# A two-layer backbone on one core: two PSUM banks for the by-token products, products with the gate made ahead, and longer planned steps

## The chip, the cores and the metric

One core of one Trainium2 chip runs the whole forward pass in one launch. The metric is the device time of that core in microseconds (us), lower is better. TensorE (PE) does the matrix products, VectorE (DVE) and GpSimd (POOL) the elementwise work, ScalarE (ACT) activations and copies; SyncE (SP) and ACT issue the DMAs.

## The reference, cut to what matters

The model has one even and one odd layer over 256 latent and 256 context tokens of width 2048. Everything is float32. The even layer, in which the whole change lies, is

```
p = h @ w_in                                  # 50 column blocks of 128
a, r, k, v, wd, ad, gate = split(p)
mixed = [pool_mixer(a) | rwkv7(r, k, v, wd, ad), both directions]
y = (mixed * silu(gate)) @ w_out
x = layer_norm(alpha * x + gate_l * y)
```

`rwkv7` is a recurrence over the tokens for 16 heads of 64, in both directions: S becomes S*w + (S a) b + v k, and the output is S r. The odd layer is attention with the same frame. Products of activations and weights run as three float32r matmuls (high*high, high*low, low*high) on operands that were split into a high and a low part.

## The kernel before, in words

**Matrix order.** The order of TensorE's instructions is written by a planner at build time (`merge`, line 121). Work is a set of generators with priorities. A generator that yields a number asks to go on that many planned microseconds later; one that yields another generator waits for its end. The planner keeps a planned clock `self.t`, which `mm` and `tp` move on, and always takes the first ready generator in the order of priority. The last in priority, the fill (`fill0`, line 1303), is the projection with weights that has no dependence: it runs in every planned wait of the others. The order of the other engines and of the DMA queues is chosen by the framework from its own simulated timeline.

**The fill.** `inproj` (line 321) makes one block of 128 columns of p: four units of 12 matmuls of 128x512. `run_fill` (line 183) loads the weights of a unit on SP (`load`, line 198), up to `rawbufs` - 1 units ahead, and splits them one unit ahead (`split`, line 203: ACT makes whi, POOL makes wlo). A block that is done goes to DRAM (`spill`, line 299); the 16 gate blocks pass SiLU first. The order of the blocks is r, k, v by pairs of heads, then the 8 pool blocks, then the 16 gate blocks 0 to 15.

**The recurrence** (`rwkv`, line 1272) goes through 8 passes of two heads each. `lora` (line 358) makes the decay rates once, `prep` (411) the operands of a pass, `gram` (484) the products within a chunk of 64 tokens, `inverse` (542, on DVE) and `join` (577) the inverse of a triangular block, `by_token` (504) the transposed operands and NV, and `chain` (628) the recurrence itself in 8 chunks. While `chain` of pass p runs, `prep` and `inverse` of pass p + 1 run beside it; `join` and `by_token` of p + 1 follow when the chain has ended. `readout` (675) ends a pass and writes `mixd` to DRAM; the last pass runs beside `pools` (696), the pooling mixer.

**PSUM.** There are eight banks: two each under the names acc, tr and prep, one each under cx and cz. `chain` uses cx and cz; `join`, `gram` and `by_token` share the two tr banks. A bank is given out again when all that it held has been read.

**Out-projection of the even layer** (`out0`, line 893). When the fill's blocks are done, `gate_acts` (880) makes for each of 16 blocks k, in the order `korder` (8 to 14, 0 to 7, 15), the product of `mixd` and the gate: two loads on SP, a multiplication on DVE (line 743) and a split, hh on ACT and hl on POOL (`split_act`, 76; `gated_act`, 734), in turn in the two ev tiles and in two raw tiles. `outproj` (860) runs passes of 16 units of 12 matmuls; pass 0 uses the acc and tr banks and takes block k when it is there. When pass 0 has ended, `done` (916) waits for the recurrence and calls `pools()` (897), which closes the memory pools of the recurrence and of ev, opens the larger set of weight buffers (`rawbufs` from 4 to 6) in their place and calls `loads(0)`: six DMAs of 256 KB on ACT for the layer norm. `done` then uses them and calls `loads(1)`, six more.

Of the kernel before, what the change touches and what calls it, by code (L numbers as in the profile page):

```python
# [7 lines left out]
F32 = mybir.dt.float32  # L8
F32R = mybir.dt.float32r
AF = mybir.ActivationFunctionType  # L10
ALU = mybir.AluOpType
# [3 lines left out]
KT = D // 128  # L15
# [13 lines left out]
M_A, M_R, M_K, M_V, M_WD, M_AD, M_G = 0, 8, 16, 24, 32, 33, 34  # L29
# [7 lines left out]
class Kern:  # L37
# [320 lines left out]
    def lora(self):  # L358


        nc, io = self.nc, self.io
        rows = (slice(0, 64), slice(64, 128))
        W, xh = [], [self.rt([128, 2, 512], f"AR{j}", F32R, bufs=2) for j in range(2)]
        xl = [self.rt([128, 2, 512], "BKT0", F32R), self.rt([128, 2, 512], "BK", F32R, bufs=2)]
        for j in range(2):
            nc.gpsimd.memset(xl[j][rows[1 - j]].bitcast(F32), 0.0)
        stage = [("GN0", None), ("BKT1", None), ("GR0", 2), ("GR1", 2)]
        raws = []
        for j, m in enumerate((M_WD, M_AD)):
            for d in range(2):  # L370
                t = self.rt([128, 2, 512], "M")[:, :, 0:258] if j + d == 0 else self.rt([128, 2, 512], "GN1")[:, :, 0:258] if j + d == 2 else self.rt([128, 8, 65], "P").rearrange("p a b -> p (a b)")[:, 0:516].rearrange("p (s t) -> p s t", s=2) if j else self.rt([128, 2, 258], "rsh")
                nc.gpsimd.memset(t[:, :, 0:258:257], 0.0)
                for r in rows:
                    nc.sync.dma_start(t[r, :, 1:257], self.pd[m][rows[d], :].rearrange("p (s t) -> p s t", s=2))
                raws.append(t)
        t1 = self.rt([128, 2, 512], "D")
        for j, n in enumerate(("w2", "a2")):
            hi, lo = rows[j], rows[1 - j]
            for d in range(2):
                w = self.rt([128, 1024], stage[2 * j + d][0], bufs=stage[2 * j + d][1])  # L380
                nc.scalar.dma_start(w, io[n][d])
                Wt = self.rt([128, 1024], ("X", "U0", "U1", "NV")[2 * j + d], F32R)
                W.append(Wt)
                x = self.rt([128, 512], "acc", bufs=2)
                self.shifted(raws[2 * j + d], d, self.c("mul", 2 * j + d), self.muc[:, 48 + 2 * j + d:49 + 2 * j + d], x.rearrange("p (s t) -> p s t", s=2), t1[:, d, :])
                if j == 0:
                    nc.scalar.activation(x, x, AF.Tanh)
                nc.scalar.copy(xh[j][:, d, :], x)
                nc.vector.tensor_tensor(out=xl[j][hi, d, :], in0=x[hi], in1=xh[j][hi, d, :].bitcast(F32), op=ALU.subtract)
                nc.scalar.copy(Wt, w)  # L390
                (nc.vector if d else nc.gpsimd).tensor_tensor(out=Wt[lo], in0=w[lo], in1=Wt[lo].bitcast(F32), op=ALU.subtract)
        outs = [self.rt([128, 2, 512], n, bufs=b) for n, b in (("GN0", None), ("BKT1", None), ("GN1", None), ("GR0", 2), ("GR1", 2))]
        yield 12.0
        for p in range(8):
            ps = slice(p * 128, p * 128 + 128)
            for d in range(2):
                o = outs[(2 * p + d) % 5]
                for j, b in enumerate(("w0", "a0")):
                    pw = self.pt(("prep", "tr")[j])
                    self.mm(pw, W[2 * j + d][:, ps], xh[j][:, d, :], stop=False)  # L400
                    self.mm(pw, W[2 * j + d][:, ps], xl[j][:, d, :], start=False)
                    last = nc.scalar.activation(o[:, j, :], pw, AF.Sigmoid, bias=self.c(b, d * 8 + p))
                    yield 0.2
                nc.sync.dma_start(self.sgd[p, d], o)
                self.rates += 1
        self.preload(last)
# [97 lines left out]
    def by_token(self, st):  # L504

        nc, cst = self.nc, self.cst
        st["U"] = U = [self.rt([128, 2, 8, 64], f"U{h}") for h in range(2)]
        st["BKT"] = BKT = [self.rt([128, 16, 64], f"BKT{h}") for h in range(2)]
        st["NV"] = NV = self.rt([128, 2, 8, 64], "NV")
        for d in range(2):  # L510
            pv = self.pt("tr", (128, 8, 64))
            for c in range(8):
                for h in range(2):
                    hs = slice(64 * h, 64 * h + 64)
                    os = slice(64 - 64 * h, 128 - 64 * h)
                    self.mm(pv[os, c, :], st["v"][d][hs, c * 64:c * 64 + 64], cst["cen"][hs, :], share=0.5)
            with self.tc.high_priority():
                nc.scalar.copy(U[0][64:128, d], pv[64:128])
                nc.vector.tensor_copy(U[1][0:64, d], pv[0:64])
            yield 0.5  # L520
        for d in range(2):
            pq = [self.pt("tr", (128, 8, 64)) for _ in range(2)]
            for c in range(8):
                for h in range(2):
                    hs = slice(64 * h, 64 * h + 64)
                    self.tp(pq[h][:, c, :], st["BK"][d][hs, c, :, :], cst["ident"][hs, hs], share=0.5)
            with self.tc.high_priority():
                for h in range(2):
                    (nc.scalar.copy if h else nc.vector.tensor_copy)(BKT[h][:, d * 8:d * 8 + 8, :], pq[h])
            yield 1.8  # L530
        for d in range(2):
            pn = self.pt("tr", (128, 8, 64))
            for c in range(8):
                for h in range(2):
                    ks = slice(64 - 64 * h, 128 - 64 * h)
                    os = slice(64 * h, 64 * h + 64)
                    self.mm(pn[os, c, :], st["GN"][h][ks, d * 8 + c, :], U[h][ks, d, c, :], share=0.5)
            with self.tc.high_priority():
                nc.scalar.copy(NV[:, d], pn)
            yield 1.2  # L540
# [82 lines left out]
                lo = slice(64 * h, 64 * h + 32)  # L623
                (nc.scalar.copy if h else nc.vector.tensor_copy)(X[lo, :, 1, :], px[lo])

    LAG = 1.7, 2.4, 2.2

    def chain(self, st):

# [100 lines left out]
                nc.scalar.activation(ev, ps, AF.Identity, scale=self.c("pscale", 2 * g + m))  # L730
                nc.sync.dma_start(self.mixd[2 * g + m], ev)


    def gated_act(self, k):

        nc = self.nc
        if self.korder.index(k) % 2:
            g, x = (self.ep.tile([128, 512], F32, tag="ev", name="ev") for _ in range(2))
        else:
            g, x = (self.rt([128, 2, 258], f"raw{j}").rearrange("p a b -> p (a b)")[:, 0:512] for j in range(2))  # L740
        nc.sync.dma_start(g, self.pd[M_G + k])
        nc.sync.dma_start(x, self.mixd[k])
        nc.vector.tensor_tensor(out=x, in0=x, in1=g, op=ALU.mult)
        return self.split_act(x, 512)

    def rsqrt(self, pool, out, v):

# [129 lines left out]

        return self.run_fill([unit(j, i, k) for j in range(len(passes)) for i, k in enumerate(ks)])

    def gate_acts(self):  # L880
        last = None
        for k in self.korder:
            yield self.mixed[k]
            yield from self.spilled(M_G + k)
            y = self.gated_act(k)
            yield 2.6
            if last is not None:
                self.y[last[0]] = last[1]
            last = k, y
        yield 2.0  # L890
        self.y[last[0]] = last[1]

    def out0(self, main):
        nc, io = self.nc, self.io
# [13 lines left out]
        def loads(n):  # L908
# [4 lines left out]
            for t in range(4):  # L913
                self.behind(nc.scalar.dma_start(z[t][:, w], io["xtok"][t * 128:(t + 1) * 128, w]), after)

        def done(n, toks, acc):
            if n == 0:
                yield main
                yield self.gemv_p
                pools()  # L920
            for t, a in zip(toks, acc):
                w = slice(n * 512, n * 512 + 512)
                tmp = self.ln.tile([128, 512], F32, tag="tmp", name="tmp", bufs=2)
# [23 lines left out]
        a, b = ("acc", "acc", "tr", "tr"), ("prep", "prep", "cx", "cz")  # L947
# [355 lines left out]
    def fill0(self, main):  # L1303

        right = lambda name, **kw: self.tc.tile_pool(name=name, side="right", **kw)
        rkv = [m + p for p in range(1, 8) for m in (M_R, M_K, M_V) if m + p != M_R + 1]
        yield from self.run_fill([u for m in rkv + list(range(8)) + [M_G + i for i in range(16)] for u in self.inproj(m)])
        self.act.__exit__(None, None, None)
        self.act2 = right("act2", bufs=KT)
        self.hp = self.act2.__enter__()  # L1310
        self.spawn(self.gate_acts(), 5)
        yield from self.out0(main)
        yield from self.layer1()

    def run(self, ctx):
        tc, self.ctx = self.tc, ctx
        self.joined = Proc(None, 0, 0)
        self.mixed = [Proc(None, 0, 0) for _ in range(KT)]
        self.y = [None] * KT
        self.there = set()  # L1320
        self.rates = 0
        self.bns = {}
# [2 lines left out]
        with tc.manual_schedule(engines={mybir.EngineType.PE}):  # L1325
# [5 lines left out]
            self.lo_pat = "p"  # L1331
            main = self.spawn(self.rwkv())
            self.gemv_p = self.spawn(self.gemvs(), 8)
            fill = self.spawn(self.fill0(main), 9)
            self.merge(main, fill)

# [72 lines left out]
```

## Time and profile before

| | us |
|---|---|
| median of 3 runs (lowest, highest) | 1929.61 (1924.73, 1929.91) |
| the profiled execution's own time | 1930.54 |
| its span, first to last instruction | 1928.8 |
| PE busy in it | 1734.2 (90%) |
| DVE, ACT, POOL busy | 1026.6, 730.0, 667.3 |
| mean granted clock of PE, as a share of the full one | 0.95 |

The span is what the trace shows; the profiled execution took 1.7 us more. A matmul's record lasts longer than the time after which the next one starts, so a busy PE is not yet PE at its peak; idle PE and a lower granted clock are both lost time.

### The profile page before, as it was taken

How to read it: one execution, taken by the hardware profiler on the slowest of the kernel's cores; microseconds unless marked ns; L12 is line 12 of the kernel's file. 1: busy time of each engine (PE TensorE's matmuls, PEld its weight loads, DVE VectorE, ACT ScalarE, POOL GpSimd, SP SyncE). 2: the span in 40 equal slices, each digit the busy share in tenths (PEclk: the TensorE clock that was granted, in tenths of full speed). 3: DMA queues.
4: the chain of work that ended last, by engine and by line, in shares of the span. 5: the costliest groups of instructions: out<-in, count | busy, mean ns of one | idle time of the engine just before them, and what ended most of it. 6: DMA issues, size and time to landing. Idle time of an engine off the chain costs nothing. (4 is left out here: it accounts for less than half of the span.)

```text
span 1928.8 us, 38942 instructions
## 1 busy us (share of the span) xinstructions
PE 1734.2 (90%) x15584; PEld 1299.8 (67%) x15584; DVE 1026.6 (53%) x1983; ACT 730.0 (38%) x1402; POOL 667.3 (35%) x574
## 2 busy tenths in 40 slices
PE   6887999898989898989888999889998999999994
PEld 3665666666666666666655778658776878888773
DVE  1223456575858484858443111241296387667458
ACT  1115633333333334242213333322363455555444
POOL 1113334141414141424232444654646332221234
PEclk8888999898999898999799999989999999999998
DMA  9886844353534453534444533664553453443754
GB/s 368 306 295 199 296 145 147 124 168 119 159 120 145 134 176 121 162 125 134 128 151 163 187 125 121 191 204 126 164 191 126 148 153 115 126 137 98 244 189 163
DMA packets 162213, 322.72 MB, mean 167 GB/s; under 512 B 17648, under 2 KB 28400, under 8 KB 160880
## 3 DMA queue, kind: packets, MB, share of 16 engines
q1 hardware_dynamic: 153680, 299.15, 47.8%
q10 hardware_dynamic: 8352, 21.09, 3.4%
q8 instruction: 122, 2.00, 0.4%
q14 instruction: 59, 0.48, 0.1%
HBM read 290.25 MB, written 29.92 MB: 166 GB/s over the span
## 5 line engine op out<-in xcount | busy, mean ns | idle before, releaser
L74 POOL TENSOR_TENSOR wlo<-wrow,whi 128x512 fp32r<-128x512 f32 (+1 forms) x348 | 473.5, 1363 | 921.9 <-ACT whi L206 805.4
L206 ACT CAST whi<-wrow 128x512 fp32r<-128x512 f32 (+1 forms) x528 | 328.2, 625 | 604.7 <-PE acc L87 223.0
L87 PE MATMUL acc<-hh,whi 128*128 128x512 f32 (+1 forms) x992 | 384.8, 388 | 9.5 <-ACT whi L206 9.5
L87 PE MATMUL acc<-hh,wlo 128*128 128x512 f32 (+1 forms) x992 | 385.5, 389 | 8.7 <-POOL wlo L74 5.1
L87 PE MATMUL acc<-hl,whi 128*128 128x512 f32 (+1 forms) x992 | 385.5, 389 | 0.0
L87 PEld LDWEIGHTS acc<-hh,wlo 128*128 128x128 f32 x992 | 191.4, 193 | 55.2 <-issue 11.1
L87 PEld LDWEIGHTS acc<-hh,whi 128*128 128x128 f32 x992 | 191.9, 193 | 53.8 <-ACT whi L206 13.4
L87 PEld LDWEIGHTS acc<-hl,whi 128*128 128x128 f32 x992 | 191.0, 193 | 41.8 <-issue 10.8
L74 DVE TENSOR_TENSOR wlo<-wrow,whi 128x512 fp32r<-128x512 f32 (+1 forms) x180 | 143.3, 802 | 133.8 <-ACT whi L206 133.1
L87 PE MATMUL tr<-wlo,hh 128*128 128x512 f32 x224 | 91.7, 409 | 6.8 <-POOL wlo L74 3.7
L87 PE MATMUL tr<-whi,hl 128*128 128x512 f32 x224 | 90.9, 406 | 0.0
L87 PE MATMUL tr<-whi,hh 128*128 128x512 f32 x224 | 90.1, 402 | 0.0
L87 PE MATMUL prep<-gw,sc 128*32 128x128 f32 x2048 | 80.5, 291 | 5.8 <-DMA gw<-in_modB 3.8
L316 DVE TENSOR_SCALAR ev<-ev 128x512 f32<-128x512 f32 x16 | 17.5, 1094 | 106.6 <-ACT ev L315 106.6
L87 PEld LDWEIGHTS prep<-gw,sc 128*32 128x32 f32 x2048 | 53.8, 114 | 17.4 <-issue 6.9
L87 PE MATMUL acc<-whi,hh 128*128 128x512 f32 x128 | 52.5, 410 | 5.2 <-ACT hh L78 4.8
L87 PE MATMUL acc<-whi,hl 128*128 128x512 f32 x128 | 53.4, 417 | 3.7 <-POOL hl L74 3.5
L87 PEld LDWEIGHTS tr<-wlo,hh 128*128 128x128 f32 x224 | 42.8, 191 | 19.2 <-POOL wlo L74 5.1
L461 POOL TENSOR_TENSOR BK<-T,D 64x512 f32<-64x512 f32 x32 | 46.5, 1453 | 25.8 <-DVE T L456 22.1
L87 PE MATMUL prep<-wrow,sc 128*32 128x256 f32 x512 | 38.4, 436 | 17.8 <-DMA wrow<-in_modA 17.8
L87 PE MATMUL acc<-wlo,hh 128*128 128x512 f32 x128 | 52.3, 409 | 2.0 <-POOL wlo L74 1.2
L87 PEld LDWEIGHTS tr<-whi,hh 128*128 128x128 f32 x224 | 42.8, 191 | 10.6 <-issue 0.5
(362 smaller groups left out, 3113.4 us busy)
## 6 DMA issues: line engine op xcount, KB each, us to landing
gw<-in_modB SPq DMA_DIRECT2D x256, 256.0 KB
wrow<-in_wA SPq DMA_DIRECT2D x176, 256.0 KB
wrow<-in_modA SPq DMA_DIRECT2D x64, 512.0 KB
wrow<-in_w SPq DMA_DIRECT2D x112, 256.0 KB
wrow<-in_woA SPq DMA_DIRECT2D x80, 256.0 KB
wrow<-in_wo SPq DMA_DIRECT2D x80, 256.0 KB
wrow<-in_w1g SPq DMA_DIRECT2D x64, 256.0 KB
pd<-ev SPq DMA_DIRECT2D x50, 256.0 KB
```

Of the source, the lines that this page charges most:

```text
L74: e.tensor_tensor(out=out, in0=raw, in1=hi.bitcast(F32), op=ALU.subtract)
L87: self.nc.tensor.matmul(out, a, b, start=start, stop=stop)
L206: self.lastsplit = self.nc.scalar.copy(hi, raw)
L316: nc.vector.tensor_scalar(out, out, 1e30, 1.0, op0=ALU.min, op1=ALU.add)
L461: nc.gpsimd.tensor_tensor(out=BK[hs, :, 1 - h, :], in0=c8(k)[hs], in1=c8(ew)[hs], op=ALU.mult)
```

## The change

It has five parts. (1) `lora` asks for a planned 16 us in place of 12 before its matmuls. (2) `by_token` puts its three groups of products into cx and cz, which `chain` has left at that point, in place of the tr banks; the copies of one direction's v product are both made by one engine (ACT for direction 0, DVE for 1) where ACT and DVE had one half each. (3) `LAG`, the planned waits in each of the chain's 8 steps, goes from 1.7, 2.4, 2.2 to 2.2, 2.6, 2.6 us. (4) The products with the gate leave `gate_acts` for a new generator `gated_acts`, which starts when the recurrence has ended, while the fill still runs, and puts the 16 products into the freed AR and GR tiles; the gate blocks are projected in `korder`; `gate_acts` only splits, with hl on DVE and POOL in turn, and asks for 1.3 us per block in place of 2.6. (5) `pools()` is called by a generator of its own as soon as the recurrence, the modulation vectors and `gate_acts` have ended, in the middle of pass 0, in place of its end.

```diff
@@ lora
-        yield 12.0
+        yield 16.0
@@ by_token
-            pv = self.pt("tr", (128, 8, 64))
+            pv = self.pt(("cx", "cz")[d], (128, 8, 64), 1)
...
-                nc.scalar.copy(U[0][64:128, d], pv[64:128])
-                nc.vector.tensor_copy(U[1][0:64, d], pv[0:64])
+                e = nc.vector.tensor_copy if d else nc.scalar.copy
+                e(U[0][64:128, d], pv[64:128])
+                e(U[1][0:64, d], pv[0:64])
...
-            pq = [self.pt("tr", (128, 8, 64)) for _ in range(2)]
+            pq = [self.pt(t, (128, 8, 64), 1) for t in ("cx", "cz")]
...
-            pn = self.pt("tr", (128, 8, 64))
+            pn = self.pt(("cx", "cz")[d], (128, 8, 64), 1)
@@ chain
-    LAG = 1.7, 2.4, 2.2
+    LAG = 2.2, 2.6, 2.6
@@ gate_acts
-    def gate_acts(self):
-        last = None
-        for k in self.korder:
+    def gated_acts(self, main):
+
+        nc = self.nc
+        yield main
+        t = None
+        for n, k in enumerate(self.korder):
             yield self.mixed[k]
             yield from self.spilled(M_G + k)
-            y = self.gated_act(k)
-            yield 2.6
+            if n % 2 == 0:
+                t = self.rt([128, 2, 512], ("AR0", "AR1", "GR0", "GR1")[n // 2 % 4], bufs=2)
+            x = t[:, n % 2, :]
+            g = self.rt([128, 2, 258], f"raw{n % 3}").rearrange("p a b -> p (a b)")[:, 0:512]
+            nc.sync.dma_start(g, self.pd[M_G + k])
+            nc.sync.dma_start(x, self.mixd[k])
+            nc.vector.tensor_tensor(out=x, in0=x, in1=g, op=ALU.mult)
+            yield 3.0
+            self.prod[k] = x
+
+    def gate_acts(self):
+
+        last = None
+        for n, k in enumerate(self.korder):
+            while k not in self.prod:
+                yield 0.5
+            y = self.split_act(self.prod[k], 512, "vp"[n % 2])
+            yield 1.3
             if last is not None:
                 self.y[last[0]] = last[1]
             last = k, y
-        yield 2.0
+        yield 1.5
@@ out0
+        def change():
+            for p in (main, self.gemv_p, self.acts):
+                yield p
+            pools()
+
+        change = self.spawn(change(), 5)
+
         def done(n, toks, acc):
             if n == 0:
-                yield main
-                yield self.gemv_p
-                pools()
+                yield change
@@ fill0
-        yield from self.run_fill([u for m in rkv + list(range(8)) + [M_G + i for i in range(16)] for u in self.inproj(m)])
+        yield from self.run_fill([u for m in rkv + list(range(8)) + [M_G + k for k in self.korder] for u in self.inproj(m)])
@@ run
+            self.spawn(self.gated_acts(main), 6)
```

## Rows read from the trace of the kernel before

**Rows 1.** The page, part 1: busy time of the engines.
```profile
PE 1734.2 (90%) x15584; PEld 1299.8 (67%) x15584; DVE 1026.6 (53%) x1983; ACT 730.0 (38%) x1402; POOL 667.3 (35%) x574
```
**Rows 2.** Stretches: us, busy PE, PEld, DVE, ACT, POOL (count), clock, DMA share, GB/s.
```profile
250.00:1045.00 795.00, 712.50 (x10302) 511.52 (x10291) 504.83 (x1041) 270.93 (x553) 239.80 (x233) 0.93 0.45 142
1045.00:1212.00 167.00, 167.00 (x857) 131.07 (x855) 30.81 (x35) 62.19 (x106) 72.33 (x56) 1.00 0.45 145
1212.00:1270.00 58.00, 49.10 (x182) 34.75 (x182) 20.92 (x19) 19.43 (x34) 41.14 (x31) 0.94 0.66 200
1270.00:1284.00 14.00, 6.23 (x24) 4.35 (x23) 8.51 (x14) 1.14 (x2) 1.93 (x2) 0.78 0.98 273
1284.00:1300.00 16.00, 15.39 (x60) 12.31 (x60) 3.19 (x8) 3.10 (x5) 8.20 (x7) 0.87 0.49 161
1300.00:1326.00 26.00, 26.00 (x113) 20.90 (x112) 0.00 (x0) 5.58 (x9) 11.63 (x9) 1.00 0.38 104
```
**Rows 3.** Waits of PE, 215 to 1045 us: total us, times, longest.
```profile
PE tr L87 <- issue: 17.6, 10, 3.2
PE cx L87 <- DVE R L648: 10.8, 7, 2.7
PE tr L101 <- ACT T L614: 8.5, 5, 1.8
...
PE cz L87 <- DVE S L666: 5.5, 4, 1.8
PE cz L87 <- DVE U L654: 5.1, 4, 3.3
...
PE tr L87 <- DVE BKT L529: 3.1, 2, 2.0
PE tr L101 <- DVE U L519: 3.0, 3, 1.3
```
**Rows 4.** Timeline in pass 6's join and by_token: start, us, engine, line [idle before].
```profile
744.99 1.33 ACT L345 ACTIVATE M<-raw,muc 128x512 f32<-128x512 f32 x2 [1.30 <-PE tr L87]
...
746.35 0.58 ACT L614 COPY T<-tr 32x512 f32<-32x512 f32 x1
...
746.98 0.80 PE L101 MATMUL tr<-cc,BK 64*128 64x64 f32 x10 [1.83 <-ACT T L614]
```
**Rows 5.** Groups by line: count, busy us, mean ns, idle before and its releaser.
```profile
L519 DVE COPY U<-tr 64x512 f32<-64x512 f32 x16 | 10.9, 682 | 35.1 <-ACT U L518 35.0
...
L518 ACT COPY U<-tr 64x512 f32<-64x512 f32 x16 | 9.3, 581 | 42.7 <-PE tr L87 42.7
```
**Rows 6.** Timeline in lora.
```profile
180.61 1.26 POOL L74 TENSOR_TENSOR wlo<-wrow,whi 128x512 fp32r<-128x512 f32 x1 [0.35 <-PE acc L87]
...
185.11 0.76 PE L87 MATMUL tr<-AR,U 128*128 128x512 f32 x1 [4.64 <-ACT AR L388]
```
**Rows 7.** Timelines: the recurrence's last store; the fill's last recorded block matmul.
```profile
1061.17 0.33 SPq L694 DMA_DIRECT2D mixd<-acc  x1
...
1211.60 0.40 PE L87 MATMUL acc<-hh,wlo 128*128 128x512 f32 x1
```
**Rows 8.** Tile hl, then waits of PE, 1212 to 1300 us.
```profile
L74 POOL TENSOR_TENSOR hl<-raw,hh x8: 1262/1281/1450, 1213.8 to 1265.7; 128x512 fp32r<-128x512 f32 x8
...
PE prep L87 <- ACT whi L206: 7.8, 1, 7.8
PE acc L87 <- ACT hh L78: 4.8, 2, 3.3
PE acc L87 <- POOL hl L74: 3.5, 5, 1.0
```
**Rows 9.** Timelines of SP and ACT around the end of pass 0.
```profile
1270.00 29.93 SPq L200 DMA_DIRECT2D wrow<-in_woA  x12
...
1275.93 6.52 ACTq L914 DMA_DIRECT2D z<-in_xtok  x4
1282.55 0.62 ACT L206 CAST whi<-wrow 128x512 fp32r<-128x512 f32 x1 [12.98 <-DMA wrow<-in_woA]
```

More of the change, by code (lines that the diff above doesn't have):

```diff
@@ L731, in pools @@
                 nc.sync.dma_start(self.mixd[2 * g + m], ev)
[L734 to L744, printed above, removed]
     def rsqrt(self, pool, out, v):
@@ L878, in outproj @@
         return self.run_fill([unit(j, i, k) for j in range(len(passes)) for i, k in enumerate(ks)])
+    def gated_acts(self, main):
[3 more added lines that the diff above has]
+        for n, k in enumerate(self.korder):
+            yield self.mixed[k]
+            yield from self.spilled(M_G + k)
+            if n % 2 == 0:
[7 more added lines that the diff above has]
+            self.prod[k] = x
     def gate_acts(self):
         last = None
-        for k in self.korder:
-            yield self.mixed[k]
-            yield from self.spilled(M_G + k)
-            y = self.gated_act(k)
-            yield 2.6
+        for n, k in enumerate(self.korder):
[3 more added lines that the diff above has]
+            yield 1.3
             if last is not None:
@@ L1310, in fill0 @@
         self.hp = self.act2.__enter__()
-        self.spawn(self.gate_acts(), 5)
+        self.acts = self.spawn(self.gate_acts(), 5)
         yield from self.out0(main)
@@ L1318, in run @@
         self.mixed = [Proc(None, 0, 0) for _ in range(KT)]
-        self.y = [None] * KT
+        self.y, self.prod = [None] * KT, {}
         self.there = set()
```

## The prediction

> **What bounds the kernel now.** I read the busy times first: TensorE is busy for 1734.2 of 1928.8 us and no other engine comes near [rows 1]. The change neither adds nor removes a matmul, so all it can win is idle TensorE and time at a lower clock. The view by stretches shows where these lie [rows 2]. From 1045 to 1212 us, where only the fill runs, TensorE is never idle and the clock is full: nothing can be won there. From 250 to 1045 us, the recurrence, it is idle for 795 - 712.5 = 82.5 us and the mean clock is 0.93, so a further 0.07 x 795 = 56 us of clock is missing. From 1212 to 1284 us, pass 0 of the out-projection and its end, 8.9 + 7.8 us are idle, at clocks of 0.94 and 0.78. The waits of TensorE tell what ended the idle times [rows 3, 8]. The rest of the kernel is not touched.
>
> **The frame: what covers a longer recurrence.** Parts 1 and 3 make the recurrence longer, and the fill is what runs in its planned waits. Before, the recurrence's last store is at 1061.2 us and the fill's last matmul at 1211.6 [rows 7], so 150 us of fill are left behind its end. A step of the chain grows by 0.5 + 0.2 + 0.4 = 1.1 us, 0.9 in the first; 8 passes of 8 steps give about 8 x 8.3 = 66 us, and lora 4. The 16 products with the gate, at a planned 3 us each, need 48 more. 66 + 4 + 48 = 118 of 150: all stays under the fill, with 32 us to spare, and the last product waits for the last gate block in any case. I therefore count the growth itself at nothing; without that cover it costs 1 us per us.
>
> **Part by part.**
>
> *Lora.* TensorE waits 4.64 us for ACT at 185.1 [rows 6]. Four planned us more put a unit of fill ahead of lora's matmuls. That unit's wlo is only made at 180.6 to 181.9 [rows 6], so part of the wait stays. Between 0 and 4.6 I take 4, including some clock.
>
> *By-token products in cx and cz.* In the tr banks, a product of by_token waits until join's product two places before it has been copied out, and the other way round. The row at 747 us shows it: the second transposition group waits 1.83 us for ACT's copy of join's T, which itself stood behind two activations of the next prep [rows 4]. These waits are 8.5 us (ACT T) and 3.1 us (DVE BKT) over the passes [rows 3]. Both go, since each user now waits for its own copies alone: 11.6 us. What does not go is the wait for the copies of U, 3.0 us [rows 3]: the transpositions still need the banks of the v products. What is late next is the pair of DVE copies of direction 1, behind join's DVE work; at 0.68 us each [rows 5] it could cost up to 1.4 us in 8 passes, 11 us, which would give the whole term back. By this bound and by the 3.0 us also going the term lies between 0 and 14.6; I take 11.6, because DVE is busy for only 505 of 795 us there [rows 2].
>
> One engine now makes both copies of a v product: 2 x 0.58 us on ACT, 2 x 0.68 on DVE. Before, the DVE copy waited for the ACT copy 35.0 us in all [rows 5], so the two ran one after the other, 0.58 + 0.68 us, and nothing is lost. The Trainium skill, page "PSUM — Partial Sum Buffer", section "PSUM bank collisions raise a hardware error", says that two engines may work on different quadrants of one bank at the same time, and these halves are different quadrants; by it the split copies could take 0.68 us and the change would lose about 0.5 us on each of 16 products, 8 us. The trace speaks against that for this kernel: the order is in the program.
>
> *Longer steps.* The chain's products wait for DVE's R, S and U: 10.8 us in 7 waits, 5.5 in 4 and 5.1 in 4 [rows 3]. A longer planned wait takes at most its own growth from each: 7 x 0.5 + 4 x 0.4 + 4 x 0.2 = 5.9 us. I take 6. Below it is bounded by nothing (DVE late by as much again), above by the 21.4 us of the rows.
>
> *Clock in the recurrence.* 56 us of clock are missing there; the stages with no idle TensorE have the full clock [rows 2]. With 17.6 of 82.5 us of idle time gone, a fifth, I would expect a fifth of the 56, 11 us; since the waits for issue, 17.6 us in 10 [rows 3], stay, I take 8, between 0 and 25.
>
> *Pass 0.* Its 16 units of 12 matmuls take 26.00 / 113 = 0.23 us each where nothing waits [rows 2], 44.2 us; the stretch has 58. POOL makes hl and wlo, 2 x 1.28 us per unit or more [rows 8], on loads that come in the same moment, and TensorE waits 4.8 + 3.5 us for hh and hl. With the products ready and every other hl on DVE, POOL has 1.9 us of work per unit of 2.8. The first hh and hl still have to be made, about 3.5 us. Gain 58 - 44.2 - 3.5 = 10 us, between 5 and 13. The 32 loads on SP move to where DMA is at 0.45 and TensorE has no wait [rows 2]; three units of weights, 8 us, are in hand there, so they cost nothing; a queue that sits behind a gate's store for longer than that would cost the rest.
>
> *The change of pools.* Now the first weight load into the new buffers is issued at 1270.0, and its whi comes at 1282.55; TensorE waits 7.8 us [rows 8, 9]. The DMA engines are at 0.98 in that stretch, since both groups of six loads on ACT run with it [rows 2, 9]. Missing clock adds 14 x 0.22 + 16 x 0.13 = 5 us. In the middle of pass 0 only one group runs beside the weights, so about half the 12.5 us, against two to three units of 2.8 us in hand: up to 1 us of wait, and some clock if ACT sits behind the last hl. Of 13 us I take 8, between 0 and 13.
>
> **Sum.** 4 + 11.6 + 6 + 8 + 10 + 8 = 47.6 us. From the profiled execution's 1930.5 that gives 1882.9; that execution is 0.9 us above the median of the runs, which does not matter here. I predict 1883.
>
> **The rivals.**
>
> *The stall of the pool change only moves.* The same six loads, the same weights and the same engines meet some 30 us earlier, and `loads(1)` follows at the end of the pass. For it: DMA at 0.98 [rows 2]. Against: half the bytes at a time. The time is 1883 + 8 = 1891. The Trainium skill, page "Trainium Kernel Development and Optimization", section "Key Constraints", says that DMAs from SP and ACT run on the same 16 DMA engines and interleave, so a second queue saves only the time of issue; by that rule this rival holds.
>
> *The recurrence gives its part back.* Bursts of small matmuls come closer together and wait for issue, DVE's two copies come late, and no clock returns. Then lora (4), the steps (6) and pass 0 (10) stay: 1930.5 - 20 = 1910.5. For it: issue waits are the largest row of the recurrence [rows 3]. Against: they lie within single bursts, whose number stays.
>
> *The recurrence becomes the bound.* If steps grow by more than planned, for instance because longer passes push inverse and join back as well, the products come after the fill's end and pass 0 waits for them. It decides once the recurrence and products use more than the 150 us behind it [rows 7], 32 us beyond the sum above; each further us costs one. Steps longer by 2.7 us in place of 1.1 (64 x 1.6 = 102 us more) would give 1883 + 102 - 32 = 1953, slower than now. Against: chain and prep now end together only if nothing else limits a pass, and the growth is written down.
>
> *The change does not do what it says*, where the framework puts the early loads and products late on SP and DVE: pass 0 and the pools then gain nothing, 1883 + 18 = 1901.
>
> **How the numbers follow.** The forecast has a chance of 0.55, the moved stall 0.15, the recurrence giving back 0.17, the late products 0.07, the recurrence as the bound 0.04, and 0.02 for no effect. The range goes down to 1850, where the steps, the clock and the pools reach towards their upper bounds, and up to 1911, the second rival. A measurement of this kernel can tell about 0.3%, 6 us. Every case but the last two is faster by more: 0.94 faster, 0.02 within, 0.04 slower.
>
> **What would show it.** Right: no wait of the transpositions for ACT T and of join for BKT; fewer and shorter waits of cx and cz for R, S, U; a mean clock above 0.94 from 250 us to the recurrence's end, which comes some 20 to 60 us later than now; products on DVE before the fill's end; pass 0 in under 49 us; a wait for whi of under 3 us at the new place of the pools. Wrong: new waits of TensorE on cx and cz in by_token of more than 1 us per pass; idle TensorE ahead of pass 0; the 7.8 us again in mid-pass.

## The result and the profile after

The changed kernel takes 1879.88 us (median of 4 runs, 1878.91 to 1888.00) against 1929.76 us for the kernel before in the same comparison (4 runs, 1924.73 to 1933.20): a ratio of 0.9752, 95% interval 0.9723 to 0.9781. The prediction was 1883 with a range of 1850 to 1911. The profiled execution took 1879.39 us with a span of 1877.6.

The page of the kernel after, part 1, answers to [rows 1]:

```profile
PE 1711.6 (91%) x15584; PEld 1286.9 (69%) x15584; DVE 1048.8 (56%) x1992; ACT 728.6 (39%) x1402; POOL 660.8 (35%) x565
```

The matmuls are as many as before. The span is 51.2 us shorter: PE's busy time falls by 22.6 us, because fewer of its matmuls run at the lower clock, and its idle time by 28.6, from 194.6 to 166.0.

The view by stretches of the kernel after (columns as in [rows 2]):

```profile
250.00:1107.00 857.00, 795.11 (x10848) 575.65 (x10847) 538.72 (x1071) 305.87 (x615) 279.76 (x264) 0.96 0.49 156
1107.00:1172.00 65.00, 65.00 (x280) 52.30 (x279) 16.77 (x18) 24.62 (x42) 30.90 (x24) 1.00 0.49 155
1172.00:1190.00 18.00, 4.16 (x12) 2.54 (x11) 14.73 (x11) 9.95 (x19) 13.22 (x9) 0.63 0.14 44
1190.00:1236.00 46.00, 45.07 (x184) 35.59 (x183) 8.00 (x15) 9.62 (x16) 19.93 (x15) 0.96 0.53 152
```

In the recurrence PE is idle for 857 - 795.1 = 61.9 us where it was 82.5, and the clock is 0.96 where it was 0.93. The fill behind its end (second line) is still at full clock without a gap. The new loss is in the third line: at the start of pass 0 PE does 4.16 us of work in 18.

Where the 51 us came from, by four marks that both traces have (us from the span's start):

| mark | before | after | stage ending there |
|---|---|---|---|
| first block of the fill copied out | 152.5 | 151.0 | -1.5 |
| first matmul of pass 0 | 1213.5 | 1174.6 | -37.4 |
| first matmul of pass 1 | 1272.5 | 1236.5 | +2.9 |
| first `tmp` product behind pass 1 | 1326.4 | 1279.5 | -10.9 |
| last instruction | 1928.7 | 1877.5 | -4.3 |

The first and the last line are untouched code; their 5.8 us are no gain of the change. The part of the last line behind the attention's last q tile lasts 184.2 us before and 178.8 after, and 179.6 to 183.4 in the twelve other kernels below, so the two profiles happen to be its extremes.

The waits of PE from 250 to 1107 us in the kernel after (columns as in [rows 3]):

```profile
PE cz L87 <- DVE U L655: 12.1, 6, 6.4
PE cx L87 <- DVE S L667: 11.0, 10, 1.7
...
PE cz L101 <- DVE U L520: 3.0, 3, 1.4
...
PE cz L101 <- DVE D L568: 2.7, 1, 2.7
PE cz L87 <- DVE R L649: 2.4, 2, 1.3
...
PE cx L87 <- DVE BKT L530: 0.8, 1, 0.8
```

The transpositions' wait for ACT's T, 8.5 us in [rows 3], is gone; BKT fell from 3.1 to 0.8. The wait for the copies of U is 3.0 us as before. R fell from 10.8 to 2.4, but S rose from 5.5 to 11.0 and U from 5.1 to 12.1.

And from 1172 to 1300 us, against the second half of [rows 8]:

```profile
PE acc L87 <- DVE ev L319: 11.8, 1, 11.8
PE acc L87 <- ACT hh L78: 1.5, 1, 1.5
PE acc L87 <- POOL wlo L74: 0.9, 1, 0.9
PE acc L87 <- DVE hl L74: 0.5, 1, 0.5
```

The waits for hh, hl and whi shrank to 2.0 us. One that was not there before has their place: 11.8 us for L319, the last step of a gate block's SiLU. The timeline of the kernel after, ACT and DVE, shows what it stood behind (start, us, then the number of instructions at the end):

```profile
1173.49 0.59 ACT L315 ACTIVATE ev<-acc 128x512 f32<-128x512 f32 x1
1173.98 2.17 ACT L78 CAST hh<-AR 128x512 fp32r<-128x512 f32 x4
1174.12 1.09 DVE L316 TENSOR_SCALAR ev<-ev 128x512 f32<-128x512 f32 x1 [1.41 <-ACT ev L315]
...
1181.24 0.63 ACT L317 ACTIVATE ev<-ev 128x512 f32<-128x512 f32 x1
...
1182.28 0.63 ACT L318 ACTIVATE ev<-ev 128x512 f32<-128x512 f32 x1
...
1184.12 3.42 DVE L74 TENSOR_TENSOR hl<-GR,hh 128x512 fp32r<-128x512 f32 x2
...
1187.46 0.67 DVE L319 TENSOR_TENSOR ev<-ev,acc 128x512 f32<-128x512 f32 x1
```

The product loads and the products themselves begin earlier than the planner's order says: DVE makes the first at 981.5 us, before the recurrence has ended. The SiLU of the last gate block reads its acc bank at the first step (L315) and at the last (L319), so the bank is free only when the chain ends. Its second activation could start at 1175.21, when L316 ended, but ACT makes the hh casts of the products first: 6.0 us. L319 could start at 1182.91, but DVE is busy with hl until 1187.5: 4.6 us. Pass 0 wants that bank at once. Each profile, here and below, is of one execution.

### The profile page after: what moved, and what is told of

It reads as the page before. It is cut to its first block, busy times and chain, and to the rows that moved or that the text cites. A ratio compares the mean times of both kernels' runs of the same rounds, so it can differ in the third digit from the quotient of the medians.

```text
span 1877.6 us, 38910 instructions
## 1 busy us (share of the span) xinstructions
PE 1711.6 (91%) x15584; PEld 1286.9 (69%) x15584; DVE 1048.8 (56%) x1992; ACT 728.6 (39%) x1402; POOL 660.8 (35%) x565
## 5 line engine op out<-in xcount | busy, mean ns | idle before, releaser
L87 PEld LDWEIGHTS prep<-gw,sc 128*32 128x32 f32 x2048 | 53.4, 113 | 17.6 <-issue 7.8
L87 PE MATMUL acc<-whi,hh 128*128 128x512 f32 x128 | 52.1, 407 | 13.4 <-DVE ev L319 11.8
L461 POOL TENSOR_TENSOR BK<-T,D 64x512 f32<-64x512 f32 x32 | 46.4, 1451 | 23.2 <-PE cz L87 11.8
L87 PEld LDWEIGHTS tr<-whi,hl 128*128 128x128 f32 x224 | 42.5, 190 | 9.9 <-issue 0.7
```

The lines of the kernel that those rows point to most:

```text
L87: self.nc.tensor.matmul(out, a, b, start=start, stop=stop)
L461: nc.gpsimd.tensor_tensor(out=BK[hs, :, 1 - h, :], in0=c8(k)[hs], in1=c8(ew)[hs], op=ALU.mult)
```

## The experiments

The theory: the banks cx and cz for the products of `by_token` (part 2) bring most of it, through shorter sections between two chains and the clock that these give back; longer steps add some; pass 0's gain is eaten by the wait for the SiLU; the stall at the change of pools came from the late products and not from where the pools change. The rivals are in the expectations. Ratios are to the kernel before on the same chip, whose medians were 1926.24 (26 runs), 1924.60 (11) and 1928.05 (11); 1% is 19.3 us.

**The parts alone.** Part 2 alone, on the kernel before:

```diff
-            pv = self.pt("tr", (128, 8, 64))
+            pv = self.pt(("cx", "cz")[d], (128, 8, 64), 1)
...
-                nc.scalar.copy(U[0][64:128, d], pv[64:128])
-                nc.vector.tensor_copy(U[1][0:64, d], pv[0:64])
+                e = nc.vector.tensor_copy if d else nc.scalar.copy
+                e(U[0][64:128, d], pv[64:128])
+                e(U[1][0:64, d], pv[0:64])
...
```

The banks of `pq` and `pn` change in the same way.

> Part 2 alone on the kernel before: the by-token products in cx and cz, all else as before. Theory (each part brings its own term): waits of the transpositions for ACT T and of join for BKT go, 11.6 us, and a little clock with them; 1912 to 1920 us. Rival (the parts need each other: cx and cz are left too late by the chain with its short planned waits): new waits on cx and cz in by_token take the place of the old ones, 1925 to 1935 us.

Measured: 1895.39 us, ratio 0.9858 [0.9817, 0.9899], 27 us of gain. That is more than the theory expected, and the rival falls. From 250 us to the recurrence's last store, first the kernel before, then this one:

```profile
250.00:1061.00 811.00, 728.50 (x10407) 523.21 (x10396) 510.94 (x1048) 279.12 (x567) 244.94 (x237) 0.93 0.45 143
250.00:1029.00 779.00, 713.52 (x10413) 514.86 (x10402) 507.80 (x1048) 278.33 (x569) 243.76 (x237) 0.96 0.46 149
```

With as many matmuls in it the stretch is 32 us shorter: PE is idle for 17.0 us less and, at a clock of 0.96 in place of 0.93, busy for 15.0 us less. Part 3 alone:

```diff
-    LAG = 1.7, 2.4, 2.2
+    LAG = 2.2, 2.6, 2.6
```

> Part 3 alone on the kernel before: the longer planned waits of the chain's steps. Theory: 6 us from the waits for R, S and U and some clock; 1915 to 1923 us, and the recurrence ends some 60 us later with no cost. Rival (it is the longer pass, not the banks, that takes the waits of join and by_token away, since DVE has ended the inverse by then): 1895 to 1910 us. Third: nothing, DVE is late by as much again; 1927 to 1933 us.

Measured: 1912.96 us, ratio 0.9924 [0.9892, 0.9956], 15 us, between the theory and its rival. Neither mechanism accounts for it. R waits nearly went, but S and U waits grew, and the wait for ACT's T is longer than before, 11.9 us, so the longer pass does not take join's waits away. What fell is a wait for issue, 17.6 us in [rows 3]; from the waits of PE in this kernel, 250 to 1117 us:

```profile
PE tr L87 <- issue: 5.1, 4, 2.1
```

Why it fell, no run shows. Parts 4 and 5 alone are the kernel after with lora, the steps and the whole of `by_token` as they were:

```diff
-        yield 16.0
+        yield 12.0
...
-    LAG = 2.2, 2.6, 2.6
+    LAG = 1.7, 2.4, 2.2
...
-            pv = self.pt(("cx", "cz")[d], (128, 8, 64), 1)
+            pv = self.pt("tr", (128, 8, 64))
...
```

> Parts 4 and 5 alone on the kernel before: products with the gate made ahead, gate blocks in the order of use, the pools changed in the middle of pass 0. Theory (after the trace of the changed kernel: the split of all blocks on DVE holds up the SiLU of the last gate block, whose acc bank pass 0 wants): a wait of TensorE of about 12 us at the start of pass 0 is here as well, and no wait at the pool change; 1918 to 1926 us. Rival (that wait is an accident of the shifted recurrence): no such wait, pass 0 and 1 some 18 us shorter; 1908 to 1914 us.

Measured: 1922.28 us, ratio 0.9978 [0.9951, 1.0005]: 4 us that can't be told from nothing, as the theory said. The waits of PE from 1195 to 1320 us of this kernel have the same new wait:

```profile
PE acc L87 <- DVE ev L319: 11.5, 1, 11.5
```

Part 1 alone:

```diff
-        yield 12.0
+        yield 16.0
```

> Part 1 alone on the kernel before: lora asks for 16 us in place of 12. Theory: 0 to 5 us from the wait for ACT at 185 us and the low clock behind it; 1925 to 1930 us. Rival (the part brings nothing by itself, and only shifts the whole order): within 3 us of before.

Measured: 1918.44 us, ratio 0.9966 [0.9940, 0.9992], 7 us, more than theory or rival said. The four ratios alone add up to 1.42 + 0.76 + 0.22 + 0.34 = 2.74%, against 2.48% for the whole; the difference is within their intervals.

**Taking parts out of the whole.** The steps back to what they were, then `by_token` back in the tr banks, then lora back:

```diff
-    LAG = 2.2, 2.6, 2.6
+    LAG = 1.7, 2.4, 2.2
```

> The changed kernel with part 3 undone (planned waits 1.7, 2.4, 2.2). Theory (the parts overlap: part 2 alone took 33 us out of the stretch up to the out-projection, the whole change 37): 3 to 8 us slower than the changed kernel, ratio 0.977 to 0.979. Rival (the parts add up): as much slower as part 3 alone was faster, 13 us, ratio 0.982.

Measured: 1881.58 us, ratio 0.9781 [0.9751, 0.9812]. That is 0.29% or 6 us slower than the change, as the theory said, but the intervals overlap. Waits of PE, 250 to 1028 us of this kernel:

```profile
PE cx L87 <- DVE R L649: 9.5, 7, 2.1
...
PE cz L87 <- DVE S L667: 4.6, 4, 1.6
```

R waits are long again and S waits short: the longer steps take waits from R, and in the whole change S and U have them back.

```diff
-            pv = self.pt(("cx", "cz")[d], (128, 8, 64), 1)
+            pv = self.pt("tr", (128, 8, 64))
...
```

> The changed kernel with part 2 undone (by-token products in the tr banks, copies split between ACT and DVE). Theory (overlap: parts 1 and 3 alone took 17 and 24 us out of the stretch up to the out-projection): 8 to 15 us slower than the changed kernel, the waits for ACT T back with 8 to 12 us; ratio 0.979 to 0.983. Rival (the parts add up): 31 us slower, ratio 0.991.

(`pq`, `pn` and the copies of U are as before, too.) Measured: 1902.18 us, ratio 0.9883 [0.9848, 0.9918], 1.31% or 25 us slower than the change, nearly as much as part 2 brings alone: nearer to the rival, by which the parts add up, than to the theory. From the waits of PE in this kernel, 250 to 1135 us:

```profile
PE tr L101 <- ACT T L614: 12.0, 7, 1.8
```

And the view by stretches of this kernel for the same time:

```profile
250.00:1135.00 885.00, 814.09 (x10874) 587.58 (x10872) 539.87 (x1077) 309.07 (x617) 281.10 (x267) 0.94 0.47 151
```

The wait for ACT's T is back, and with it a clock of 0.94: with the other four parts still in, the clock of the recurrence goes with this one. (The profiled execution took 1909.01 us, the longest of this kernel's six, so its clock stands at the low end.)

```diff
-        yield 16.0
+        yield 12.0
```

> The changed kernel with part 1 undone (12 planned us). Theory (it is worth its own place: the busy time of TensorE from 153 to 215 us back from 53.6 to 50.7 us, the clock from 0.94 to 0.89): 5 to 8 us slower than the changed kernel. Rival (what part 1 alone brought, 8 us, came from shifted passes): within 3 us of the changed kernel.

Measured: 1884.10 us, ratio 0.9783 [0.9751, 0.9816], 6 us slower than the change by the ratios, as the theory said, with overlapping intervals. The stretch of lora, 153 to 215 us, in the kernel with the longer wait alone:

```profile
153.00:215.00 62.00, 54.48 (x268) 38.86 (x267) 16.18 (x15) 44.87 (x67) 19.21 (x20) 0.94 0.89 306
```

And in the change without the longer wait:

```profile
153.00:215.00 62.00, 50.61 (x242) 34.91 (x241) 14.19 (x14) 42.84 (x65) 17.41 (x19) 0.86 0.85 290
```

The like pairs are the first line with the kernel before, where PE is busy for 50.65 us at a clock of 0.89, and the second with the kernel after, 53.58 us at 0.94. The longer wait goes with 3.8 and 3.0 us more work in the same 62 us.

**Pass 0 and the pools.** Pass 0 begins in the other four banks, which no gate block uses:

```diff
-        passes = [(0, range(4), a), (1, range(4), b), (2, range(4), a), (3, (0, 1), b[:2]), (3, (2, 3), b[2:])]
+        passes = [(0, range(4), b), (1, range(4), a), (2, range(4), b), (3, (0, 1), a[:2]), (3, (2, 3), a[2:])]
```

> The changed kernel with the banks of the out-projection's passes exchanged: pass 0 in prep, cx and cz, pass 1 in acc and tr, and so on, so that pass 0 does not want the acc bank that the SiLU of the last gate block still reads. Theory: the wait of 11.8 us at the start of pass 0 goes, and with it the low clock behind it (17 us at half clock); 15 to 20 us faster than the changed kernel, a ratio to the kernel before of 0.965 to 0.968. Rival (the split itself is the limit: the first hl on DVE and POOL take 1.75 us each, side by side): TensorE waits for hl in place of the bank, at most 4 us are won, ratio 0.973 or more.

Measured: 1870.87 us, ratio 0.9717 [0.9684, 0.9750], 7 us better than the change by the ratios: between the theory's 15 to 20 and the rival's 4. Waits of PE from 1165 to 1300 us:

```profile
PE prep L87 <- POOL wlo L74: 3.0, 1, 3.0
...
PE prep L87 <- DVE hl L74: 0.5, 1, 0.5
```

The SiLU still ends late, but nobody waits for it. From its first matmul to that of pass 1, pass 0 takes 50.6 us here, 61.9 in the change and 59.0 before: of the 11.3 us saved 9.8 are idle PE and 1.5 busy PE. The theory counted the low clock on top of the wait, but PE was idle in most of the 17 us at half clock, and idle time is not lost twice. What is left is mostly a wlo that POOL makes behind the hl of the products. So I asked for more time between the products, with pass 0 still in the other banks:

```diff
-            yield 1.3
+            yield 2.4
```

> The changed kernel with the banks of the passes exchanged, and with 2.4 planned us per split block in place of 1.3. Theory (with the exchanged banks the remaining wait is wlo on POOL behind seven hl): the framework spreads the splits, the wait of 3.0 us for wlo goes, 2 to 4 us faster than the exchanged banks alone, ratio 0.969 to 0.971. Rival (the order of the other engines does not follow the planner's pace): the same as the exchanged banks alone, 0.972.

Measured: 1871.35 us, ratio 0.9716 [0.9682, 0.9749], the same: the wait for wlo stayed, 4.2 us in 3, the longest 3.0. The planned pace does not set POOL's order. Another way round is to leave DVE to the SiLU:

```diff
-            y = self.split_act(self.prod[k], 512, "vp"[n % 2])
+            y = self.split_act(self.prod[k], 512, "p")
```

> The changed kernel with every hl of pass 0 on POOL in place of DVE and POOL in turn. Theory (the last gate block's SiLU is held up twice, by hh copies on ACT for 6 us and by hl on DVE for 5 us): the wait of pass 0 for the acc bank falls from 11.8 to about 6 us, POOL's hl take 1.28 us each in place of 1.7, and wlo on POOL becomes the next wait, some 5 us; the total within 5 us of the changed kernel. Rival (DVE alone holds the SiLU up): the wait falls to under 2 us.

Measured: 1871.41 us, ratio 0.9718 [0.9678, 0.9758], 7 us better than the change by the ratios, where within 5 was expected; the intervals overlap. Its waits of PE from 1160 to 1300 us:

```profile
PE acc L87 <- DVE ev L319: 6.8, 1, 6.8
```

Of 11.8 us, DVE's share of 5 is gone and ACT's of 6 to 7 is left: the two hold-ups in the timeline are both real, and they add. The wait for wlo is 1.5 us, where some 5 were expected. The change of pools goes back to the end of pass 0:

```diff
-        change = self.spawn(change(), 5)
...
-                yield change
+                yield main
+                yield self.gemv_p
+                yield self.acts
+                pools()
```

> The changed kernel with part 5 undone: pools() again at the end of pass 0. Theory: both groups of loads on ACT run together again beside the first weights in the new buffers, TensorE waits about 8 us for whi at the end of pass 0 and loses some clock; 8 to 13 us slower than the changed kernel, ratio 0.979 to 0.982. Rival (the stall was due to the late products, whose loads and tiles held the space; these are early now): within 4 us of the changed kernel.

Measured: 1878.66 us, ratio 0.9762 [0.9725, 0.9799], the same as the change. From 1170 to 1300 us its waits of PE are, line for line, the four of the kernel after, none for whi. But the theory was not put to the test, since its condition did not come about: the loads did not move with the call. The timeline of this kernel:

```profile
1190.61 1.28 POOL L74 TENSOR_TENSOR hl<-GR,hh 128x512 fp32r<-128x512 f32 x1
1191.92 0.85 ACTq L920 DMA_DIRECT2D gb<-gated  x2
...
1226.44 0.82 ACTq L920 DMA_DIRECT2D gb<-gated  x2
```

And of the kernel after:

```profile
1194.71 1.28 POOL L74 TENSOR_TENSOR hl<-GR,hh 128x512 fp32r<-128x512 f32 x1
...
1196.06 0.82 ACTq L920 DMA_DIRECT2D gb<-gated  x2
...
1231.12 0.82 ACTq L920 DMA_DIRECT2D gb<-gated  x2
```

In both the first group of loads on ACT is issued when the last product's hl has ended (1191.89 and 1195.99), and the second group some 35 us later. So part 5 brings nothing once part 4 is there, and this run says nothing on what two groups together would cost. In the kernel before, the first weight load into the new buffers is issued at 1270.00 [rows 9]; the last hl that reads an ev tile runs from 1268.69 to 1269.98 there, and `pools()` closes the pool of the ev tiles just before it opens that of the new buffers. With the products early, their last reader ends early in pass 0; with parts 4 and 5 alone it ends at 1229.82 and the loads begin at 1229.85. That the release comes from these tiles is read from the times; no run isolates it, and in the kernel before the loads on ACT begin at 1267.05 already.

How full the DMA engines are beside the first group, the kernel after shows (columns as in [rows 2]):

```profile
1196.00:1210.00 14.00, 13.92 (x61) 10.86 (x59) 0.49 (x3) 2.39 (x4) 3.88 (x4) 1.00 0.93 287
```

The share is 0.93, against 0.98 in the stretch from 1270 to 1284 before [rows 2], but PE is idle for 0.08 us only.

**The copies of U.** By one engine per half again, in the new banks:

```diff
-                e = nc.vector.tensor_copy if d else nc.scalar.copy
-                e(U[0][64:128, d], pv[64:128])
-                e(U[1][0:64, d], pv[0:64])
+                nc.scalar.copy(U[0][64:128, d], pv[64:128])
+                nc.vector.tensor_copy(U[1][0:64, d], pv[0:64])
```

> The changed kernel with the copies of each v product split again between ACT and DVE, all else as changed. Theory (the program puts the two halves one after the other): the DVE copy waits for the ACT copy as before, no gain; within 4 us of the changed kernel or up to 8 us slower, since the second copy on each product is late by the change of engine. Rival (the halves lie in different quadrants of a bank and run side by side, 0.68 us in place of 1.2 or 1.4): 4 to 8 us faster than the changed kernel.

Measured: 1869.74 us, ratio 0.9726 [0.9691, 0.9761], 5 us better than the change by the ratios, though the intervals overlap. That is in the rival's range, but not by its mechanism. From the timeline of this kernel in pass 4:

```profile
666.77 0.58 ACT L518 COPY U<-cx 64x512 f32<-64x512 f32 x1 [1.36 <-PE cx L87]
667.38 0.68 DVE L519 COPY U<-cx 64x512 f32<-64x512 f32 x1 [2.98 <-ACT U L518]
```

DVE begins its half 0.61 us after ACT has begun its own, which takes 0.58. So the two halves still run one after the other, as in [rows 5]. The gain, if it is one, seems to come from DVE's order: with the change, both copies of direction 1 stand behind join's work on DVE; with halves, only one of each product does. In pass 4 of the kernel after they start at 669.14 and 669.85, behind join's transposition that ends at 669.11, and PE is idle for 1.15 us before the transpositions into cz; with halves for 0.26. That this is the whole of the 5 us is not shown. The view by stretches gives the sections from the first v product to the last NV product. First the kernel before: passes 1, 4 and 5 (counted from 0), and the sum over all eight:

```profile
361.10:381.70 20.60, 17.50 (x471) 13.53 (x470) 9.36 (x14) 9.91 (x16) 2.31 (x3) 0.75 0.29 85
642.40:664.50 22.10, 17.96 (x473) 13.81 (x472) 9.44 (x15) 8.80 (x14) 1.86 (x3) 0.77 0.32 105
732.90:757.20 24.30, 18.98 (x471) 14.90 (x470) 9.73 (x15) 8.80 (x14) 1.99 (x3) 0.72 0.20 61
sum 172.90, PE 135.79 PEld 104.49 DVE 76.20 ACT 64.20 POOL 16.05; mean PE 16.97 PEld 13.06 DVE 9.53 ACT 8.03 POOL 2.01
```

The same view of the kernel after, for the same passes:

```profile
369.30:384.00 14.70, 13.35 (x471) 10.81 (x470) 9.41 (x14) 7.32 (x13) 2.00 (x3) 1.00 0.48 145
663.30:683.30 20.00, 17.60 (x472) 14.21 (x471) 9.53 (x15) 8.80 (x14) 2.24 (x3) 0.74 0.32 106
764.40:784.70 20.30, 17.67 (x473) 13.78 (x472) 9.82 (x16) 8.51 (x14) 1.03 (x2) 0.75 0.30 91
sum 141.00, PE 123.14 PEld 98.78 DVE 83.04 ACT 61.05 POOL 16.42; mean PE 15.39 PEld 12.35 DVE 10.38 ACT 7.63 POOL 2.05
```

And of the kernel with the copies by halves:

```profile
372.40:386.90 14.50, 13.70 (x471) 11.07 (x470) 9.25 (x14) 7.64 (x14) 2.02 (x3) 1.00 0.47 147
665.60:680.50 14.90, 13.46 (x472) 11.17 (x472) 9.40 (x15) 7.32 (x13) 2.19 (x3) 1.00 0.42 136
760.50:775.10 14.60, 13.77 (x473) 11.22 (x473) 9.62 (x16) 7.62 (x13) 1.04 (x2) 1.00 0.41 129
sum 128.00, PE 115.98 PEld 93.65 DVE 81.66 ACT 60.21 POOL 16.45; mean PE 14.50 PEld 11.71 DVE 10.21 ACT 7.53 POOL 2.06
```

The same work takes 173, 141 and 128 us. Before, all eight sections lose clock; after, three of eight are at the full clock, and with halves five. A section at 1.00 takes some 15 us, one at 0.77 or less takes 20 or more. These are single executions, and the clock differs between executions of one kernel: the mean clock of the kernel before ranged from 0.943 to 0.961 over the eleven runs that the last ratios rest on.

Four kernels do better than the change by 8 us or more by the median: the other banks for pass 0 (1870.87, and 1871.35 with the longer pace), hl on POOL (1871.41) and the copies by halves (1869.74). Their intervals, though, overlap with its own. The other banks together with the halves, which touch different stages, were not tried.

## Why the prediction was right or wrong

The forecast of 1883 us came within some 3 us, and that is in good part luck. Up to pass 0 it had 29.6 us of gain and the traces show 37.4; for pass 0 and the pools it had 18 and they show 8.0; and 5.8 us of the difference between the two profiles are in code that nobody touched.

| term | forecast | shown by | measured |
|---|---|---|---|
| lora | 4 | alone; taken out | 7; 6 |
| by-token banks, with the clock's 8 | 11.6 + 8 | alone; taken out | 27; 25 |
| steps | 6 | alone; taken out | 15; 6 |
| pass 0 | 10 | traces, first matmul of pass 0 to pass 1 | -2.9 |
| change of pools | 8 | traces, pass 1 and its end; part 5 taken out | 10.9; nothing |

*Lora.* Right in size. The 4.6 us of waiting for ACT [rows 6] are not among the waits of the kernel after in that stretch, but part of the wait stayed, as the text said: 1.6 us for DVE's part in making the same operands (L389). All waits there fell from 11.3 to 8.2 us, and the clock rose from 0.89 to 0.94.

*By-token products.* The mechanism was right: the wait for ACT's T went, BKT almost, and the wait for U's copies stayed at 3.0 us as named; with the 2.7 us behind D, 1.2 behind modc and 0.8 behind BKT, the waits for ACT and DVE in the new banks come to 7.7 us, just under the 1 us per pass that would have spoken against it. Two waits for issue on cz, 5.1 us, come on top; on tr such waits were 17.6 us [rows 3] and are 2.1. The size was off in the clock. "A fifth of the 56, 11 us ... I take 8" shared the missing clock out over all idle time alike. The rows say that much of it hangs on these sections: part 2 alone takes 17.0 us of idle time out of the recurrence, where 11.6 were forecast, and 15.0 us of busy time at the same number of matmuls, where the clock's whole term was 8. In the change the recurrence's missing clock falls from 56 us to (1 - 0.96) x 857 = 34, and is at (1 - 0.94) x 885 = 53 when this part alone is undone, in the longest of that kernel's six executions. (The clock is shown to two digits, so each of these is good to some 4 us, and they count idle time too, in which a low clock costs nothing.)

*The copies.* The bound in the text, DVE's pair of direction 1 behind join's work, is seen in the rows; it cost about 5 us, if the difference of the two ratios is taken, which the intervals leave open. By the Trainium skill, page "PSUM — Partial Sum Buffer", section "PSUM bank collisions raise a hardware error", as cited in the prediction, the halves could have run side by side. In this kernel they do not, also in the new banks: DVE's half begins when ACT's has ended (667.38 and 667.35 us). Whether the chip would allow it, no run here shows.

*Steps.* "A longer planned wait takes at most its own growth from each" was right for R, 10.8 to 2.4 us, and the text's lower bound, DVE late by as much again, was right for S and U, which rose by 12.5 us together. In the whole change the steps bring 6 us or nothing that can be told; alone 15. The sign "fewer and shorter waits of cx and cz for R, S, U" came for R only. A step of the clock's term failed with it, that "the waits for issue, 17.6 us in 10 [rows 3], stay": with part 3 alone they fell from 19.6 to 10.4 us in all, while R, S and U together fell by 2.7 only. So the term was near for the whole change, but not by the working that gave it.

*The cover.* Right. The recurrence's last store comes at 1107.0 us, 45.8 later than before and within the 20 to 60 named, and PE has no gap from there to 1172 us. The 66 + 4 us of growth were an overestimate for the whole: part 3 alone moves that store 55.8 us back, part 2 alone brings it 32.6 forward. (The first step of a chain grows by 0.6 us and not by 0.9, since its first wait is a fixed 2.6; the sum of 8.3 has it right.) The recurrence as the bound did not come near.

*Pass 0.* This step failed: "The first hh and hl still have to be made, about 3.5 us." That is only when PE gets its operands; the acc bank was overlooked. The last gate block's SiLU still holds it, and the early products put fourteen casts on ACT (4 + 4 + 4 + 2 before the second activation) and eight hl on DVE in front of it. Before, the products were made one by one and left gaps for it: PE waited 0.4 us for that step there. The estimate of the pass itself was 3 us short: with the other banks it takes 50.6 us against 44.2 + 3.5, of which 3.5 are waits (3.0 for wlo, 0.5 for hl) and 47.1 busy time at a clock of 0.97. The term also had hl on POOL at 1.28 us; beside DVE it takes 1.71. The sign "pass 0 in under 49 us" was missed, and the sign of being wrong, "idle TensorE ahead of pass 0", came with 11.8 us.

*Change of pools.* The size was near and the mechanism held, but it was put down to the wrong part. The stall of 7.8 us is gone, and the rival by which it only moves fell, although its condition came true: the DMA engines are nearly as full beside the first group of loads, 0.93. (The rule cited for that rival, the Trainium skill, page "Trainium Kernel Development and Optimization", section "Key Constraints", has the DMAs of SP and ACT share the same 16 engines; the trace agrees, with that share.) "Up to 1 us of wait", with units in hand, was right: PE lost 0.08 us. What failed is that the change of pools brings this. The loads go when the last hl has ended, with part 5 and without it, so the 10.9 us belong to the early products of part 4. How much of the old stall was the late issue and how much the full DMA engines stays open. Before, SP issued no weight load for 8 us ahead of 1270.00, and the next took 12.5 us to its whi. A load of the same 256 KB issued at 1263.24 had released DVE at 1266.23, after 3.0 us. By an estimate from these rows, a first weight at that pace would have been there at 1273.0, ahead of the 1275.5 at which PE ran out of work, so the late issue alone need not have made the wait.

The recurrence giving its part back fell with the part alone: 0.9858, where that rival had no gain from it. (Its 1910.5 left out the 8 us of the pools without a reason; with them it is 1902.5.) That the change does not do what it says fell with the rows: the products run early (the last `mixd` load for them is issued at 1109 us, the first product's hh at 1174).

## What to carry to other kernels

When work is made early so that it is ready, look at what the same engines still owe to the buffers that the next stage needs: a bank is free at the end of its whole evacuation chain, and each step of that chain queues behind the new work. Idle time in short bursts of small matmuls can cost more than its own length, because the clock goes with it: here 17.0 us less idle time came with 15.0 us less busy time. And before a stall is put down to a busy queue, see at which instruction's end the first late transfer is issued; when a call is moved in the program, see in the trace whether its transfers moved too. Here they did not, so the run says nothing on the queue.

## What the runs showed of the hardware

A little idle time seems to decide on a section's clock. The same work, some 470 matmuls, most of them small, ran at a granted clock of 1.00 (2.4 GHz) in three sections of the changed kernel and at 0.74 to 0.75, with the lower level of 1.2 GHz in part of the stretch, in passes 4 and 5. With the copies by halves these two have 1.0 and 1.8 us less idle time and are at the full clock, at which PE is busy for 4.1 and 3.9 us less in them. That so little would go with so much had not been expected; it is seen in two sections, of one execution each.

DVE and POOL slow each other when both split. Tile hl of the kernel after (the three numbers are minimum, median and maximum ns):

```profile
L74 DVE TENSOR_TENSOR hl<-AR,hh x4: 677/1752/1760, 1175.1 to 1182.5; 128x512 fp32r<-128x512 f32 x4
...
L74 POOL TENSOR_TENSOR hl<-AR,hh x4: 1706/1710/1755, 1175.2 to 1183.6; 128x512 fp32r<-128x512 f32 x4
```

The same tile in the kernel with hl on POOL alone:

```profile
L74 POOL TENSOR_TENSOR hl<-AR,hh x8: 1262/1272/1731, 1170.7 to 1184.5; 128x512 fp32r<-128x512 f32 x8
```

DVE's first took 0.68 us, begun 0.06 us before POOL's first; from then on each takes about 1.71 to 1.75 us, where POOL alone takes 1.27. The Trainium skill, page "SBUF — State Buffer", section "Who interferes with whom", says that a DVE instruction with two SBUF inputs contends with a GpSimd instruction that reads SBUF. The trace agrees. If each blocked the other for its whole length, a pair would take 0.68 + 1.27 = 1.95 us; the pairs here take 1.71, so the two do not shut each other out quite fully. The pair makes the hl of two blocks in 1.71 us, POOL alone in 2.54.
